# One last down product in program order: the transposes of the next layer's input moved away from their norms

## The chip, the cores and the metric

The kernel runs on one core of a Trainium2 chip. The metric is the device time of one execution in microseconds; the time given is the median of several runs. The profile is of one execution on the same core, and its times count from the first instruction of the span.

## What is computed

Two layers of a causal decoder, on x of 1024 positions by 1024 features, all in float32. Layer 0 mixes tokens by dilated window attention, layer 1 by HGRN2, a gated linear recurrence. Each mixer is followed by a dense squared-ReLU MLP, and each sub-layer is applied as a post-norm:

```python
for i in range(DEPTH):                       # 2
    y = mixer(i, x)                          # attention, then hgrn2
    x = layer_norm(ALPHA * x + y, ln_mix_g[i], ln_mix_b[i])
    y = square(relu(x @ w_up[i])) @ w_down[i]        # 1024 -> 4096 -> 1024
    x = layer_norm(ALPHA * x + y, ln_ffn_g[i], ln_ffn_b[i])
```

The change lies where the first layer's MLP ends and the second layer's mixer begins: the last part of `h @ w_down`, the layer norm, and the first products `x @ w_in` of HGRN2. ("First layer" is layer 0 in the code; the text calls the two layers 1 and 2.)

## The kernel before

Each float32 product is made of three matmuls on operands that were split into a high half (a float32r copy, by ScalarE, "ACT") and a low half (the difference, by VectorE, "DVE"): high by high, high by low and low by high. They add up in one PSUM bank. Positions are cut into eight tiles of 128, tiles 0 to 3 the first half, 4 to 7 the second.

The MLP's two products save an eighth of the work by seven block products instead of eight. In `ffn` (from L1015) the down product runs over a list `steps` (L1160): six block products, each over 16 blocks j of the hidden dimension, with four tiles at a time; and last block product 3, which is done in three passes `PASS` (L1159): tiles 0 and 1 in the first pass, tile 2 in the second, tile 3 in the third. A step of the first pass is 6 matmuls (L1260, L1263, L1264 for two tiles), one of the others 3.

For each step n the loop at L1394 writes: `load_down(n + 8)`, the loads, L1169; `product_down(n)`, the matmuls, L1249; `split_down(n + 2)`, high and low halves, L1203; and `after(n)`, L1303. For block product 3 a load at L1181 brings `d`, the hidden values of several steps at once (four steps in the first pass, eight in the others), and one at L1187 `dr`, a block of the weights, in the first pass only; the split weights `dT` are kept for the other two passes. The splits of `d` are `d3s` (L1219, L1220), in a pool of three buffers; PE frees one when a step's matmuls are done.

`after(n)` adds finished products into the residual tile z (L1282) and puts follow-up work into the list `todo`, from which the next steps take one entry each (`None` is a step without work). For a tile t the follow-up is:

- `norm_of(t)` (L1291): `ln_math` (L193): statistics and scaling on DVE, two small operations and a scaling pass on ACT (L213), the bias on GpSimd (L214, "POOL"), then the store to `x3d` (L1296), issued by the queue of SyncE ("SP").
- `tr(t)` (L1286): eight transposes of z on TensorE ("PE", L223) into two PSUM banks, and four ACT copies (L233) and four DVE differences (L234) that write the tile's columns of `xn`, the split and transposed input of the next mixer. `xn[1]` holds tiles 4 to 7, `xn[0]` tiles 0 to 3; each is a group of eight SBUF buffers, asked for at the first `tr` of its half.
- `finish(t)` (L1298): both, one after the other, in a layer that isn't the last.

The mixer that follows, `hgrn` (L1482), loads its first weights by `pre` (`gw.prefetch(0)`: L142, then the split L137, L138), clears `aT` (L1485), and runs projections of 24 matmuls (L171 to L173). The first three read `xn[1]`, the next three `xn[0]`. After each projection it takes one entry of the list `late`, which the MLP returned; before, that list is empty here.

Almost all large SBUF tiles come from one pool of 50 buffers (`U`).

What sets the order. A planner reorders the instructions of every engine: it simulates the program, gives each engine the ready instruction that is written earliest, and hands out buffers. `in_order(engines)` is the kernel's way to switch this off: between its enter and its exit each instruction on these engines is tied to the one written before it on that engine, in order only and without a wait on the chip. The up product is held so on PE, DVE and SP (L1373). For the down product `in_order(())` (L1392) names no engine, so its order is the planner's throughout.

Of the kernel before, what the change touches and what calls it, by code (L numbers as in the profile page):

```python
# [62 lines left out]
def trunk_kernel(  # L63
# [32 lines left out]
    def U(name, dt=F32):  # L96
        return up.tile([P, 1024], dt, name=name, tag="u")
# [64 lines left out]
    def new_xT(half, name):  # L162
        return XT(name)
# [23 lines left out]
    def bcast_rows(ap, name):  # L187
        t = U(name)
        nc.sync.dma_start(t, ap.rearrange("(o d) -> o d", o=1).broadcast_to([P, D]))
        return t  # L190
# [45 lines left out]
    def ln_tr(t, z, xs):  # L236
        x_ = xs[t // 4]
        c = slice((t % 4) * P, (t % 4) * P + P)
        for j, pt in enumerate(z_tr(z)):
            put(x_.hi[2 * j:2 * j + 2], x_.lo[2 * j:2 * j + 2], pt, c)  # L240
# [774 lines left out]
    def ffn(li, xf, late, res, gB_ap, bB_ap, last, pre=None):  # L1015
# [143 lines left out]
        PASS = ((0, 1), (2,), (3,))  # L1159
        steps = [(i, j, (0, 1, 2, 3)) for i in ORD for j in range(NP)]  # L1160
# [3 lines left out]
        def held(n, j):  # L1164
            if (n, j // 2) not in hold:
                hold[n, j // 2] = U("hold")
            return hold[n, j // 2][:, (j % 2) * 512:(j % 2) * 512 + 512]

        def load_down(n):  # L1169
            if n >= len(steps):  # L1170
                return
            i, j, qs = steps[n]
            top, bot = w_down[li, j], w_down[li, j + NP]
            if 0 <= n - SHIFT < NP:
                nc.sync.dma_start(held(3, n - SHIFT), w_down[li, n - SHIFT][:, R])
            if i == 3:
                w = len(qs) * P
                js = 1024 // w
                if j % js == 0:
                    many[qs] = U("d3")  # L1180
                    nc.sync.dma_start(many[qs].rearrange("p (j c) -> p j c", c=w),  # L1181
                                      hd[i - 1, j:j + js, :, qs[0] * P:qs[0] * P + w].rearrange("j p c -> p j c"))
                t = many[qs][:, j % js * w:min(j % js * w + 256, 1024)]
                r = None
                if qs == PASS[0]:
                    r = U("dr3")[:, L]
                    nc.sync.dma_start(r, bot[:, R])  # L1187
                rows_[n] = t, r
                return
            two = U("dr")  # L1190
            t, r = two[:, L], two[:, R]
            nc.sync.dma_start(t, hd[i - 1, j])
            if i == 1:
                nc.sync.dma_start(held(1, j), top[:, L])
            elif i == 6:
                nc.sync.dma_start(r, bot[:, R])
            elif i in (2, 4):
                nc.sync.dma_start(r, bot[:, L])
            rows_[n] = t, r
# [66 lines left out]
        z, sb, norm, todo = {}, {}, {}, []  # L1266

        def piece(n, q):
            if (n, q // 2) not in sb:
                sb[n, q // 2] = U("sb" + n)  # L1270
            return sb[n, q // 2][:, (q % 2) * 512:(q % 2) * 512 + 512]

        def residual(q0):
            for t in range(q0, q0 + 4):
                z[t] = U("z")
                nc.sync.dma_start(z[t], res[t * P:(t + 1) * P, :])

        def mix(t, c, other):
            v.scalar_tensor_tensor(z[t][:, c], z[t][:, c], ALPHA, other, op0=ALU.mult, op1=ALU.add)

        def plus(t, c, o):
            v.tensor_add(z[t][:, c], o, z[t][:, c])  # L1282

        xn = [None, None]

        def tr(t):  # L1286
            if xn[t // 4] is None:
                xn[t // 4] = new_xT(t // 4, f"f{li}n")
            ln_tr(t, z[t], xn)

        def norm_of(t):  # L1291
            if last:
                ln_math(z[t], norm["g"], norm["b"], out[t * P:(t + 1) * P, :])
                return
            ln_math(z[t], norm["g"], norm["b"])
            nc.sync.dma_start(x3d[t * P:(t + 1) * P, :], z[t])  # L1296

        def finish(t):  # L1298
            norm_of(t)
            if not last:  # L1300
                tr(t)

        def after(n):  # L1303
            i, j, qs = steps[n]
            x_, y_ = cur.get("x"), cur.get("y")
            if j == 8 and i == 7:
                residual(4)
            if j == 8 and i == 5:
                residual(0)
            if j == 0 and i == 4:  # L1310
                norm["g"] = bcast_rows(gB_ap, "gB")
                norm["b"] = bcast_rows(bB_ap, "bB")
            if j == NP - 1:
                if i == 1:
                    for q in range(4):
                        act(piece("p1", q), x_[q], AF.Copy)
                elif i == 6:
                    for q in range(4):
                        v.tensor_add(piece("u2", q), y_[q], piece("p1", q))
                elif i == 7:  # L1320
                    for q in range(4):
                        v.tensor_add(piece("u3", q), y_[q], piece("p1", q))
                        todo.append(lambda q=q: mix(4 + q, L, piece("p1", q)))
                        todo.append(lambda q=q: mix(4 + q, R, piece("u3", q)))
                elif i == 5:
                    for q in range(4):
                        todo.append(lambda q=q: plus(4 + q, R, x_[q]))
                        todo.append(lambda q=q: mix(q, L, piece("p1", q)))
                        todo.append(lambda q=q: mix(q, R, piece("u2", q)))
                elif i == 4:  # L1330
                    for q in range(4):
                        plus(4 + q, L, y_[q])
                        todo.extend([None, lambda q=q: norm_of(4 + q), None])
                elif i == 2:
                    for q in range(4):
                        plus(q, L, y_[q])
                    if not last:
                        for q in (4, 5):
                            todo.extend([None, None, lambda q=q: tr(q), None, None])
                        todo.extend([None] * 7)  # L1340
                    else:
                        todo.extend([None] * 17)
                elif qs == PASS[0]:
                    for q in qs:
                        plus(q, R, x_[q])
                    if last:
                        todo.extend([None, lambda: finish(0), None, None, None, None, lambda: finish(1), None])
                    else:
                        todo.extend([None, lambda: tr(6), None, lambda: finish(0), None, None, None,
                                     lambda: tr(7), None, lambda: finish(1), None, None, None])  # L1350
                elif qs == PASS[1]:
                    plus(qs[0], R, x_[qs[0]])
                    todo.extend([None, lambda: finish(2)])
                    if pre:
                        todo.append(pre)
                else:
                    plus(qs[0], R, x_[qs[0]])
                    while todo:
                        f = todo.pop(0)
                        if f:  # L1360
                            f()
                    finish(qs[0])
            elif todo:
                f = todo.pop(0)
                if f:
                    f()
# [6 lines left out]
        order = in_order((mybir.EngineType.PE, mybir.EngineType.DVE, mybir.EngineType.SP, ))  # L1373
# [15 lines left out]
        low_up()  # L1389
        sum_up(4)  # L1390
        order.__exit__()
        order = in_order(())  # L1392
        order.__enter__()
        for n in range(len(steps)):  # L1394
            load_down(n + LOADDN)
            product_down(n)
            split_down(n + SPLITDN)
            if n + SPLIT3 < len(steps) and len(steps[n + SPLIT3][2]) == 1:
                split_down(n + SPLITDN + 1)
                split_down(n + SPLIT3)  # L1400
            after(n)
        order.__exit__()
        return xn, []


    def hgrn_consts():
# [75 lines left out]
    def hgrn(xs, late, consts, pre, gw):  # L1482
# [103 lines left out]
        for hd in range(8):  # L1586
# [66 lines left out]
            if hd == 0:  # L1653
                new = [[]] + new
            pend = [(pend[i] if i < len(pend) else []) + (new[i] if i < len(new) else [])
                    for i in range(max(len(new), len(pend)))]
# [14 lines left out]
    hc = hc[0]  # L1671
    gw = GateW()
    xs, late = ffn(0, xf, late, x1d, ln_ffn_g[0], ln_ffn_b[0], False, lambda: gw.prefetch(0))
    pr = Out(w_hgrn_out, "h", 1)
    oN, fill = hgrn(xs, late, hc, pr.pre, gw)
    xf, late = outproj_ln(pr, oN, fill, lambda t: x3d[t * P:(t + 1) * P, :],
                          ln_mix_g[1], ln_mix_b[1], x5d)
    ffn(1, xf, late, x5d, ln_ffn_g[1], ln_ffn_b[1], True)


# [75 lines left out]
```

## Time and profile before

| what | value |
|---|---|
| median of 3 runs | 2849.05 us |
| lowest and highest run | 2847.23 and 2850.16 us |
| the profiled execution | 2848.19 us |
| its span, first to last instruction | 2846.4 us |
| busy share of the span: PE, DVE, ACT, POOL | 97%, 73%, 51%, 4% |
| mean granted TensorE clock | 0.996 of full |
| layer 1's last block product and the first 30 matmuls of the mixer | 1693.93 to 1763.85 us of the span |

The profile has the busy time of each engine over the span, in 40 slices, by groups of instructions and in windows of choice; the timeline of each engine; its waits, with the instruction that ended each; and the SP queue, which issues the loads and stores. A row of the timeline is start, length, engine, line, operation, output and inputs, then `x` and a count, where several in a row are merged, and in brackets the idle time just before with what ended it. "PEld" is the weight load of a matmul, which overlaps other matmuls. Matmuls follow each other faster than their shown length, since they are pipelined.

### The profile page before, as it was taken

How to read it: one execution, taken by the hardware profiler on the slowest of the kernel's cores; microseconds unless marked ns; L12 is line 12 of the kernel's file. 1: busy time of each engine (PE TensorE's matmuls, PEld its weight loads, DVE VectorE, ACT ScalarE, POOL GpSimd, SP SyncE). 2: the span in 40 equal slices, each digit the busy share in tenths (PEclk: the TensorE clock that was granted, in tenths of full speed). 3: DMA queues.
4: the chain of work that ended last, by engine and by line, in shares of the span. 5: the costliest groups of instructions: out<-in, count | busy, mean ns of one | idle time of the engine just before them, and what ended most of it. 6: DMA issues, size and time to landing. Idle time of an engine off the chain costs nothing.

```text
span 2846.4 us, 40146 instructions
## 1 busy us (share of the span) xinstructions
PE 2773.5 (97%) x14280; PEld 2229.2 (78%) x14280; DVE 2065.6 (73%) x3830; ACT 1449.9 (51%) x3105; POOL 122.7 (4%) x67
## 2 busy tenths in 40 slices
PE   8999999999999989999999998999999999999998
PEld 6777777777777767888878887787887788878887
DVE  7768777776877767786686875565667787678677
ACT  5555555655555555544454434555553545454433
POOL 0000000000000003100000011111102200000000
PEclk9999999999999999999999999999999999999999
DMA  7766665766667523464483843001132455475654
GB/s 287 255 199 194 187 203 171 216 202 206 189 197 226 161 80 133 152 218 159 163 313 124 268 158 104 33 35 60 53 119 80 150 203 175 159 270 188 223 174 133
DMA packets 204936, 485.27 MB, mean 170 GB/s; under 512 B 29376, under 2 KB 43712, under 8 KB 204736
## 3 DMA queue, kind: packets, MB, share of 16 engines
q1 hardware_dynamic: 204736, 482.72, 51.3%
q8 instruction: 112, 1.84, 0.3%
q14 instruction: 88, 0.72, 0.1%
HBM read 362.82 MB, written 94.24 MB: 161 GB/s over the span
## 4 chain that ended last, share of the span: by engine, by line
PE 85%; DVE 6%; issue 3%; ACT 3%; DMA 2%; POOL 1%; SPq 0%; DVEq 0%; POOLq 0%; ACTq 0%
PE pmm L666 8%; PE pmm L668 8%; PE pmm L667 8%; PE pup L1114 7%; PE pup L1112 7%; PE pup L1113 7%; PE pdy L1260 4%; PE pdy L1264 4%; PE pdy L1263 4%; PE pdx L1263 3%; PE pdx L1264 3%; PE pdx L1260 3%; PE s L500 3%; PE o L539 2%; PE ppt L524 2%
## 5 line engine op out<-in xcount | busy, mean ns | idle before, releaser
L666 PE MATMUL pmm<-xh,H 128*128 128x512 f32 x1008 | 407.3, 404 | 13.1 <-ACT H L432 8.8
L668 PE MATMUL pmm<-xh,H 128*128 128x512 f32 x1008 | 395.6, 392 | 0.2 <-DVE H L440 0.2
L667 PE MATMUL pmm<-xl,H 128*128 128x512 f32 x1008 | 395.3, 392 | 0.0
L666 PEld LDWEIGHTS pmm<-xh,H 128*128 128x128 f32 x1008 | 190.8, 189 | 53.4 <-ACT H L432 8.8
L668 PEld LDWEIGHTS pmm<-xh,H 128*128 128x128 f32 x1008 | 189.9, 188 | 42.3 <-DVE H L440 0.9
L667 PEld LDWEIGHTS pmm<-xl,H 128*128 128x128 f32 x1008 | 190.9, 189 | 36.6
L514 ACT ACTIVATE p<-p,stats 128x128 f32<-128x128 f32 (+1 forms) x384 | 168.3, 441 | 93.6 <-DVE stats L511 93.1
L1263 PE MATMUL pdy<-dT,dS 128*128 128x512 f32 x512 | 199.2, 389 | 0.0
L1260 PE MATMUL pdy<-dT,dS 128*128 128x512 f32 x512 | 199.2, 389 | 0.0
L1264 PE MATMUL pdy<-dT,dS 128*128 128x512 f32 x512 | 199.2, 389 | 0.0
L511 DVE CUSTOM_DVE_ANT_0 p<-s,mask 128x128 f32<-128x128 f32 (+1 forms) x384 | 113.2, 347 | 67.7 <-PE s L500 58.4
L137 ACT ACTIVATE dS<-dr 128x512 fp32r<-128x512 f32 x192 | 119.6, 623 | 72.7 <-PE pdy L1264 36.6
L171 PE MATMUL pmm<-f0nh,wh 128*128 128x512 f32 x384 | 153.1, 399 | 0.0
L173 PE MATMUL pmm<-f0nh,wl 128*128 128x512 f32 x384 | 149.8, 390 | 0.0
L172 PE MATMUL pmm<-f0nl,wh 128*128 128x512 f32 x384 | 149.7, 390 | 0.0
L138 DVE TENSOR_TENSOR dS<-dr,dS 128x512 fp32r<-128x512 f32 x192 | 135.0, 703 | 16.1 <-ACT dS L137 12.3
L214 POOL TENSOR_TENSOR z<-z,bB 128x1024 f32<-128x1024 f32 x24 | 58.5, 2442 | 1686.6 <-ACT z L213 1679.8
L527 ACT ACTIVATE pts<-ppt 128x256 f32<-128x256 f32 (+1 forms) x192 | 85.4, 474 | 62.3 <-PE ppt L524 60.1
L137 ACT ACTIVATE dT<-hold 128x512 fp32r<-128x512 f32 x128 | 80.0, 625 | 69.1 <-DVE hold L1239 28.8
L1073 ACT ACTIVATE H<-wc 128x512 fp32r<-128x512 f32 x128 | 77.2, 625 | 74.6 <-DVE wc L1066 43.9
L1264 PEld LDWEIGHTS pdy<-dT,dS 128*128 128x128 f32 x512 | 96.1, 188 | 20.1
L1263 PEld LDWEIGHTS pdy<-dT,dS 128*128 128x128 f32 x512 | 96.1, 188 | 19.9
(395 smaller groups left out, 6943.3 us busy)
## 6 DMA issues: line engine op xcount, KB each, us to landing
xh<-xtd SPq DMA_DIRECT2D x110, 512.0 KB
xl<-xtd SPq DMA_DIRECT2D x110, 512.0 KB
dr<-hd SPq DMA_DIRECT2D x192, 256.0 KB
dr<-in_w_down_dram SPq DMA_DIRECT2D x128, 256.0 KB
rot<-e SPq DMA_DIRECT2D x192, 128.0 KB
wa<-in_w_up_dram SPq DMA_DIRECT2D x48, 512.0 KB
wb<-in_w_attn_dram SPq DMA_DIRECT2D x36, 512.0 KB
wa<-in_w_attn_dram SPq DMA_DIRECT2D x33, 512.0 KB
```

The costliest lines, as they stand in the source:

```text
L137: act(hi, raw, AF.Copy)
L171: nc.tensor.matmul(o, wh[:, k], xs.h(k), start=k == 0, stop=False)
L514: act(p[:, h, :n], p[:, h, :n], AF.Exp, bias=sS[:, 0, h, b:b + 1], scale=-1.0, accum_out=sS[:, 1, h, b:b + 1])
L666: nc.tensor.matmul(o, wh, hi[k // 2][:, c], start=begin and k == 0, stop=False, skip_group_check=True)
L667: nc.tensor.matmul(o, wh, lo[k // 2][:, c], start=False, stop=False, skip_group_check=True)
L668: nc.tensor.matmul(o, wl, hi[k // 2][:, c], start=False, stop=end and k == 3, skip_group_check=True)
L1112: nc.tensor.matmul(o, wh, xf.h(b, k), start=begin and k == 0, stop=False, skip_group_check=True)
L1113: nc.tensor.matmul(o, wh, xf.l(b, k), start=False, stop=False, skip_group_check=True)
L1114: nc.tensor.matmul(o, wl, xf.h(b, k), start=False, stop=end and k == 3, skip_group_check=True)
L1260: nc.tensor.matmul(o[q], h, T_[:, L], start=begin, stop=False, skip_group_check=True)
L1263: nc.tensor.matmul(o[q], h, T_[:, R], start=False, stop=False, skip_group_check=True)
L1264: nc.tensor.matmul(o[q], l, T_[:, L], start=False, stop=end, skip_group_check=True)
```

## The change

Three things, all in the first of the two layers; the program of the last layer is the same as before.

1. From the first step of block product 3's first pass, PE runs in program order. The exit of that region isn't at the end of the MLP: it is handed to the mixer as the third entry of `late`, and so comes behind the mixer's third projection.
2. `finish` is taken apart for tiles 0 to 3. The norms stay where they were. The transposes of tiles 0 and 1 move from the second pass into the third (behind its steps 3 and 8), with `pre` between them (behind step 4 instead of 3).
3. The transposes of tiles 2 and 3, which were in the third pass and behind it, become the first two entries of `late`: they come behind the mixer's first and second projection.

```diff
@@ after(n), at the end of the first pass @@
-                        todo.extend([None, lambda: tr(6), None, lambda: finish(0), None, None, None,
-                                     lambda: tr(7), None, lambda: finish(1), None, None, None])
+                        todo.extend([None, lambda: tr(6), None, lambda: norm_of(0), None, None, None,
+                                     lambda: tr(7), None, lambda: norm_of(1), None, None, None])
                 elif qs == PASS[1]:
                     plus(qs[0], R, x_[qs[0]])
-                    todo.extend([None, lambda: finish(2)])
-                    if pre:
-                        todo.append(pre)
+                    if last:
+                        todo.extend([None, lambda: finish(2)])
+                    else:
+                        todo.extend([None, lambda: norm_of(2), lambda: tr(0), pre, None, None, None, lambda: tr(1)])
                 else:
                     plus(qs[0], R, x_[qs[0]])
                     while todo:
                         f = todo.pop(0)
                         if f:
                             f()
-                    finish(qs[0])
+                    norm_of(qs[0])
@@ the loop over the steps @@
-        order = in_order(())
-        order.__enter__()
+        order = in_order((mybir.EngineType.PE,))
         for n in range(len(steps)):
+            if not last and steps[n] == (3, 0, PASS[0]):
+                order.__enter__()
             load_down(n + LOADDN)
             product_down(n)
             split_down(n + SPLITDN)
...
             after(n)
-        order.__exit__()
-        return xn, []
+        if last:
+            return
+        return xn, [lambda: tr(2), lambda: tr(3), order.__exit__]
```

## The prediction

> **What bounds the kernel now.** I read the page's busy shares first, then the stretch that the change touches in windows, then what PE waits for there, then the SP queue. Times are us from the start of the span.
>
> ```profile
> PE 2773.5 (97%) x14280; PEld 2229.2 (78%) x14280; DVE 2065.6 (73%) x3830; ACT 1449.9 (51%) x3105; POOL 122.7 (4%) x67
> ```
> ```profile
> 1693.93:1719.07 25.14, 24.43 (x113) 19.56 (x112) 19.09 (x41) 13.98 (x34) 0.00 (x0) 1.00 0.18 53
> 1719.07:1733.46 14.39, 13.11 (x65) 10.40 (x63) 9.79 (x27) 7.35 (x19) 4.91 (x3) 1.00 0.10 38
> 1733.46:1754.51 21.05, 16.70 (x73) 13.08 (x73) 15.82 (x32) 12.24 (x27) 3.07 (x2) 0.84 0.62 199
> 1754.51:1763.85 9.34, 7.81 (x39) 6.29 (x38) 4.48 (x8) 2.29 (x5) 2.36 (x1) 1.00 0.01 5
> 1763.85:1800.62 36.77, 36.77 (x165) 30.45 (x164) 13.04 (x13) 16.90 (x22) 5.44 (x2) 1.00 0.24 85
> ```
> ```profile
> 2794.21:2837.74 43.53, 43.53 (x192) 35.85 (x191) 1.97 (x3) 0.00 (x0) 1.00 0.27 79
> ```
>
> PE is busy 97% of the span, so it is the bound, and a change like this can only win PE's holes. The rows after the page's line give length, then busy time of PE, PE's weight loads, DVE, ACT and POOL, then granted clock, DMA share and GB/s (the last row, restricted to the product's bank, has no POOL). They are layer 1's last down product: first pass (16 steps of 6 matmuls), second and third pass (16 steps of 3 each), then the mixer's first 30 matmuls and the 162 after them. The last row is the same product in layer 2: 192 matmuls without a hole in 43.53, that is 0.2267 each. The mixer's are as fast (36.77 / 162 = 0.2270).
>
> ```profile
> 1698.02 1.03 PE L223 MATMUL lnpt<-ident,z 128*128 128x128 f32 x8
> 1698.81 0.48 PE L1260 MATMUL pdx<-dT,d3s 128*128 128x512 f32 x1
> ...
> 1702.08 0.73 PE L1260 MATMUL pdx<-dT,d3s 128*128 128x512 f32 x2 [0.18 <-ACT dT L137]
> ...
> 1703.84 0.71 PE L223 MATMUL lnpt<-ident,z 128*128 128x128 f32 x5
> 1705.08 0.73 PE L1260 MATMUL pdx<-dT,d3s 128*128 128x512 f32 x2 [0.53 <-ACT dT L137]
> ...
> 1730.97 1.09 PE L223 MATMUL lnpt<-ident,z 128*128 128x128 f32 x8 [1.28 <-POOL z L214]
> ...
> 1739.00 0.80 PE L1260 MATMUL pdx<-dT,d3s 128*128 128x512 f32 x1 [2.00 <-ACT d3s L137]
> ...
> 1748.10 1.10 PE L223 MATMUL lnpt<-ident,z 128*128 128x128 f32 x8 [0.84 <-POOL z L214]
> ...
> 1763.00 1.09 PE L223 MATMUL lnpt<-ident,z 128*128 128x128 f32 x8 [1.53 <-POOL z L214]
> ```
>
> One tile's eight transposes push the next matmul back by 0.79, and by 0.85 with the slightly longer gap behind it. So the time lost in each stretch is its length less its work: first pass 25.14 - 96 x 0.2267 - 2 x 0.85 = **1.7**; second 14.39 - 48 x 0.2267 - 2 x 0.85 = **1.8**; third 21.05 - 48 x 0.2267 - 3 x 0.85 = **7.6**; mixer 9.34 - 30 x 0.2267 - 0.85 = **1.7**. Together 12.8 us: all that can be won here. Tiles 0, 2 and 3 are transposed at 1730.97, 1748.10 and 1763.00, each while PE waits for POOL to finish that tile's norm: the transposes stand too close behind their norms. The largest hole is another one, the third pass's first step at 1739.00, where PE waits for the split of data that came late. The SP queue says why:
>
> ```profile
> 1690.58 6.19 SPq L1181 DMA_DIRECT2D d<-hd  x2
> 1730.94 2.68 SPq L1296 DMA_DIRECT2D x3d<-z  x2
> 1733.71 1.47 SPq L1181 DMA_DIRECT2D d<-hd  x2
> 1735.23 1.34 SPq L142 DMA_DIRECT2D wr<-in_w_hgrn_dram  x1
> ...
> 1748.07 0.33 SPq L1296 DMA_DIRECT2D x3d<-z  x1
> 1748.49 0.38 SPq L142 DMA_DIRECT2D wr<-in_w_hgrn_dram  x1
> ```
> ```profile
> 1733.71 4.80 DMA d<-hd
> ```
>
> SP stands for 34 us (from 1690.58 + 6.19 to 1730.94) at the store of tile 0, which waits for POOL; the third pass's two loads and the mixer's first weights are queued behind it. The load then takes 4.80 (the last row, from the chain of waits), to 1738.5, and its split releases PE at 1739.00.
>
> **The change part by part.** No work is added or dropped: 192 matmuls, 64 transposes, the same norms, stores and loads. Only order changes.
>
> *Tiles 0 and 1.* Their transposes leave the second pass for steps 3 and 8 of the third. Tile 0's is then due 9 matmuls into the third pass. Both norms need the end of the first pass, as before. Before, the first pass ended at 1719.07 and POOL released tile 0 just before 1730.97, 11.9 later; tile 1 needs one more POOL add of 2.4 (two in 4.71):
>
> ```profile
> 1728.55 4.71 POOL L214 TENSOR_TENSOR z<-z,bB 128x1024 f32<-128x1024 f32 x2 [47.71 <-ACT z L213]
> 1733.20 0.95 POOL L1485 MEMSET aT<- 128x1024 f32 x1
> ```
> ```profile
> L234 DVE TENSOR_TENSOR f0nl<-lnpt,f0nh 128x256 fp32r<-128x256 f32 x28 | 11.2, 419 | 6.5 <-ACT f0nh L233 6.3
> L138 DVE TENSOR_TENSOR wl<-wr,wh 128x1024 fp32r<-128x1024 f32 x3 | 3.7, 1222 | 0.7 <-ACT wh L137 0.6
> ```
>
> Now PE needs 48 x 0.2267 + 2 x 0.85 = 12.6 for the second pass and 2.0 for nine more matmuls, so it asks for tile 0 at 14.6 and for tile 1 at 14.6 + 0.85 + 3.4 = 18.9 after the first pass, where they are there at 11.9 and 14.3. The 1.28 goes. What is late next: tile 7's transposes return to their written place in the second pass, which puts 4 x 0.42 = 1.7 us of DVE in front of the norms. The margins of 2.7 and 4.6 cover it.
>
> *Tiles 2 and 3.* Tile 2 is transposed behind the mixer's first projection, tile 3 behind the second. Norm of 2 begins at the second pass's end and took 14.6 there (1733.46 to 1748.07, its store); it is now needed 12.6 (third pass with two tiles) + 24 x 0.2267 = 18.0 later. Norm of 3 took 8.5 (1754.51 to 1763.00) and is needed 2 x 5.4 + 0.85 = 11.7 after the third pass. The 0.84 and 1.53 go.
>
> *The loads.* This is the largest term and it is not in the diff. The new tile group (xn[0], eight buffers of the pool of 50) is first written by the split of tile 0's transposes. In the old text that stands ahead of the third pass's loads (they are written at step 9 of the second pass and step 1 of the third), in the new text behind both (step 3 of the third). The trace bears out that buffers are given in program order:
>
> ```profile
> 1682.83 1.14 ACT L137 ACTIVATE dT<-dr 128x512 fp32r<-128x512 f32 x2
> ...
> 1701.41 0.62 ACT L137 ACTIVATE dT<-dr 128x512 fp32r<-128x512 f32 x1
> ```
>
> POOL idles for 47.71, yet the memset of aT, which waits for no data, comes only when tile 0 is out; and ACT has a hole between the dT of the fifth step (last at 1682.83) and that of the sixth (1701.41), the first that is written behind tile 4's transposes and their group xn[1]. So I expect the loads beside the second pass's at about 1697, long before they are needed. Bounds: from 0, like layer 2's row, to a wait as long as now, worked out under the first rival. I take 0.
>
> *The pin.* In the first pass PE today fills its waits for ACT's dT with tile 5's transposes (the last five at 1703.84) and runs two L1260 ahead of the low half. In program order tile 5 comes after 48 matmuls, not 36, and L1263 must follow its own L1260. PE then meets the same dT at 1705.1 with tile 5 still to do: 0.85, and some 0.3 for the lost swaps. Cost 1.1, between 0 (if ACT, replanned, is earlier) and 2. The first pass then loses 1.7 + 1.1 = 2.8.
>
> *DVE in the third pass.* Norm of 2, two tiles' splits (3.4), eight d3s (3.4) and a weight's low half (1.22) make some 13 us in a stretch of 12.6. Layer 2's row (no wait, without transposes) is one end, 0; the other is a late split or weight, 3. I take 1.5 for this, the second pass and the first projection together, nearer to the row.
>
> *The weights.* wr is still behind tile 0, transposed at 1693.93 + 26.3 + 12.6 + 2.0 = about 1735; issue 1736, landing 4.1 later, then 1.06 + 1.22: 1742.5. The 4.1 is a later weight's time from its issue at 1748.49 to its split, which the DMA released:
>
> ```profile
> 1752.57 1.06 ACT L137 ACTIVATE wh<-wr 128x1024 fp32r<-128x1024 f32 x1 [0.51 <-DMA wr<-in_w_hgrn_dram]
> ```
> The first projection is due about 1746, so this is covered by some 3.5 us; without that cover each us would cost one.
>
> **Sum.** 12.8 lost now, 2.8 + 1.5 = 4.3 then: **8.5 us won**. What follows runs without a hole for 36.77 us and is moved as a whole. The profiled execution took 2848.19 (span 2846.4), so 2839.7; the median of the runs is 0.86 above it, and there the forecast is **2840.5**.
>
> The clock, by its row:
>
> ```profile
> 1736.50:1743.40 6.90, 4.90 (x16) 3.68 (x15) 4.17 (x11) 3.36 (x11) 0.00 (x0) 0.51 1.09 361
> ```
>
> Eight matmuls and eight transposes in it ran at half speed, some 2.3 of the third pass's 7.6 (8 x 0.2267, and 0.5 for the transposes); the forecast has no such stretch. The Trainium skill (TensorE: Matmul & The Clock Gate, Part 1) says that an idle window of about 3.4 us halves the clock, and its Part 4 that transposes do not count as busy. The longest hole here is 2.00, but between the matmuls of 1733.46 and 1739.00 lie 5.5 us with transposes alone, so the trace agrees with both together and not with Part 1 alone. By Part 1 alone a wait in the first rival would cost its length only; by both together, the 2.3 as well.
>
> **The rivals.** *The loads stay behind the stores* (the queue order of today). PE ends the second pass at about 1733 and waits until 1739.0: 5.9, and 2.3 of clock. The gain is 8.5 - 8.2, time 2849, within 0.2%. For it: SP's order is replanned and tile 0's store still has the earlier place in the text. Against: two loads written earlier than both came at 1690.58.
>
> *The mixer's weights fall behind tile 2's store*, the slower side. If the buffers for wr come only when tile 2 is out (14.6 after the second pass, 1747.7), they land at 1752, PE stands from 1746 to 1753 (7), pays 2.3 for the clock and 2 more when the second weight queues behind tile 3's store: 8.5 - 11.3, time about 2852; with the mixer's own waits for outputs (7.2, below) half as long again, about 2855. It decides from an issue of wr later than about 1746; each us later costs one. Against: today wr goes out 4 us after tile 0's transposes and 13 ahead of tile 2's store.
>
> *Half of it*: the plan of the mixer, which is not pinned and where PE now waits 7.2 us for transposes of the outputs, falls out worse by some us, or DVE is late by 3 and more. Gain 3 to 5, about 2845.
>
> ```profile
> PE opt L1568 <- DVE on L1560: 7.2, 5, 1.5
> ```
>
> **How the numbers follow.** Forecast 0.62; loads behind the stores 0.10; half of it 0.14; weights late 0.14, of which 0.10 with the mixer's longer waits. A measurement of this kernel tells about 0.2% (5.7 us) from no change: the forecast lies beyond it, the half, the queue rival and the late weights alone within. So faster 0.62 + 0.02 (the upper end of the half) = 0.64, same 0.10 + 0.12 + 0.04 = 0.26, slower 0.10. The range goes from 2835.5 (all 12.8 won, little more) to 2849.0 (the queue rival); what is left out is the late weights and a part of the unforeseen on either side.
>
> **What would show it.** Right: third-pass loads issued near 1697; no wait for POOL z at L223 in this stretch; the clock at 1.00 throughout; PE waiting for dT for 2 to 3 us in the first pass; the 72nd mixer matmul done near 1765 instead of 1773.4. Wrong: tile 0's store ahead of the loads, a wait at L171 for wh or wl, or new waits for DVE in the mixer. The whole forecast falls if buffers are not given in program order.

## The result, and the profile after

The changed kernel takes **2844.65 us** (median of 20 runs, 2842.86 to 2846.46), the kernel before 2848.45 beside it (20 runs): ratio 0.9986, 95% interval 0.998 to 0.9992. It is faster by 3.8 us, or 0.14%, where 8.5 were forecast. The time lies inside the range, and the sign was right. But the forecast, and nearly all of the 0.64 for "faster", meant a gain beyond 0.2%, and the result lies within 0.2%.

The profiled execution took 2844.54 (span 2842.8). First the page's line of busy times, then the same four stretches in windows: length, busy PE, weight loads, DVE, ACT and POOL, granted clock, DMA share, GB/s. The last window here ends with the mixer's 72nd matmul.

```profile
PE 2772.0 (98%) x14280; PEld 2229.9 (78%) x14280; DVE 2068.6 (73%) x3830; ACT 1449.2 (51%) x3105; POOL 122.7 (4%) x67
```
```profile
1694.09:1719.20 25.11, 24.44 (x113) 19.52 (x112) 19.13 (x41) 14.02 (x34) 0.00 (x0) 1.00 0.33 95
1719.20:1731.87 12.67, 12.67 (x65) 10.66 (x64) 11.17 (x29) 7.99 (x22) 3.23 (x2) 1.00 0.01 1
1731.87:1750.02 18.15, 14.77 (x66) 11.71 (x64) 13.07 (x24) 7.60 (x18) 4.76 (x3) 0.91 0.54 202
1750.02:1770.07 20.05, 18.42 (x89) 15.09 (x88) 11.42 (x18) 8.51 (x16) 2.37 (x1) 1.00 0.35 132
```

The prediction's formula (length less 0.2267 per matmul and 0.85 per tile, two tiles in each window) gives what each loses:

| stretch | before | forecast | after |
|---|---|---|---|
| first pass | 1.7 | 2.8 | 1.7 |
| second pass | 1.8 | with the next two: 1.5 | 0.1 |
| third pass | 7.6 | | 5.6 |
| mixer, first three projections | 1.7 | | 2.0 |
| sum | 12.8 | 4.3 | 9.3 |

So 3.5 us came out of the stretch, and 3.8 out of the time: what follows moved as a whole. The gain that is missing lies in the third pass and the first projections. PE's waits over the whole stretch (us in all, times, longest) and the rows of its timeline at the holes name them:

```profile
PE lnpt L223 <- DVE f0nl L234: 2.1, 1, 2.1
PE pmm L173 <- DVE wl L138: 1.6, 1, 1.6
PE pdx L1264 <- DVE d3s L138: 1.2, 1, 1.2
...
```
```profile
1733.72 0.50 PE L1264 MATMUL pdx<-dT,d3s 128*128 128x512 f32 x1 [1.23 <-DVE d3s L138]
...
1739.74 0.60 PE L223 MATMUL lnpt<-ident,z 128*128 128x128 f32 x4
1742.48 0.63 PE L223 MATMUL lnpt<-ident,z 128*128 128x128 f32 x4 [2.14 <-DVE f0nl L234]
...
1743.64 0.51 PE L1260 MATMUL pdx<-dT,d3s 128*128 128x512 f32 x1
...
1747.29 0.40 PE L1260 MATMUL pdx<-dT,d3s 128*128 128x512 f32 x1
...
1758.60 0.49 PE L173 MATMUL pmm<-f0nh,wl 128*128 128x512 f32 x1 [1.63 <-DVE wl L138]
```

No transpose waits for POOL any more; the three large holes are all waits for DVE. Yet DVE is busy for only 13.07 of the third pass's 18.15. Its own rows and POOL's, side by side, say why:

```profile
1728.64 4.74 POOL L214 TENSOR_TENSOR z<-z,bB 128x1024 f32<-128x1024 f32 x2 [47.66 <-ACT z L213]
1739.35 2.36 POOL L214 TENSOR_TENSOR z<-z,bB 128x1024 f32<-128x1024 f32 x1 [5.97 <-ACT z L213]
...
1755.09 2.37 POOL L214 TENSOR_TENSOR z<-z,bB 128x1024 f32<-128x1024 f32 x1 [12.48 <-ACT z L213]
```
```profile
1730.45 0.76 DVE L234 TENSOR_TENSOR f0nl<-lnpt,f0nh 128x256 fp32r<-128x256 f32 x2 [0.83 <-ACT f0nh L233]
1731.12 2.88 DVE L138 TENSOR_TENSOR d3s<-d,d3s 128x256 fp32r<-128x256 f32 x2
...
1739.92 2.08 DVE L138 TENSOR_TENSOR d3s<-d,d3s 128x256 fp32r<-128x256 f32 x1
1741.92 0.41 DVE L234 TENSOR_TENSOR f0nl<-lnpt,f0nh 128x256 fp32r<-128x256 f32 x1
...
1756.05 2.50 DVE L138 TENSOR_TENSOR wl<-wr,wh 128x1024 fp32r<-128x1024 f32 x1 [2.23 <-ACT wh L137]
```

A split of d normally takes 0.42. The one that starts under POOL's first pair of adds is shown for some 2.5 and ends about 0.3 after them (they end at 1733.38); another starts at 1739.92 under the next add and ends at 1742.00, also 0.3 after it (1741.71). A weight's split takes 2.50 where 1.22 is usual. "Busy" here is standing still. The differences f0nl keep their 0.4 even under POOL's adds (two in 0.76 at 1730.45): of their inputs one lies in PSUM, while both inputs of a d3s or wl lie in SBUF. The f0nl for which PE waited 2.14 had only queued behind a d3s.

The trace of before already showed this, in its third pass, under tile 2's add (POOL, DVE, and the splits of d as a group with the shortest, the median and the longest in ns):

```profile
1745.67 2.37 POOL L214 TENSOR_TENSOR z<-z,bB 128x1024 f32<-128x1024 f32 x1 [11.52 <-ACT z L213]
```
```profile
1745.93 3.07 DVE L138 TENSOR_TENSOR d3s<-d,d3s 128x256 fp32r<-128x256 f32 x3 [0.21 <-ACT d3s L137]
```
```profile
L138 DVE TENSOR_TENSOR d3s<-d,d3s x14: 406/414/2398, 1719.9 to 1751.1; 128x256 fp32r<-128x256 f32 x14
```

Three splits in 3.07 are one of 2.4 and two of 0.4. There one split was held; after the change the loads are earlier, the splits of the third pass with them, and two of d and one of a weight are held.

The Trainium skill (SBUF — State Buffer, Who interferes with whom) states this as an exclusive lock: a VectorE instruction with two SBUF inputs contends with a GpSimd instruction that reads SBUF, and the later one is blocked for the other's whole length. The traces here agree (0.42 becomes 2.08 to 2.5). It is the rule that spoke against this change, and the prediction didn't weigh it.

The SP queue after:

```profile
1690.49 12.79 SPq L1181 DMA_DIRECT2D d<-hd  x4
1731.08 10.98 SPq L1296 DMA_DIRECT2D x3d<-z  x3
1742.15 0.38 SPq L142 DMA_DIRECT2D wr<-in_w_hgrn_dram  x1
```

All four loads of d are issued by 1703.3 (1690.49 + 12.79; the forecast said about 1697), 30 us sooner than before and ahead of the stores. The mixer's weights went behind tile 2's store, as the slower rival had it, but at 1742.15 already, and PE ran the first projection without a wait for them.

### The profile page after: what moved, and what is told of

The parts are those of the page before. It is cut to its first block, busy times and chain, and to the rows that moved or that the text cites. A ratio compares the mean times of both kernels' runs of the same rounds, so it can differ in the third digit from the quotient of the medians.

```text
span 2842.8 us, 40144 instructions
## 1 busy us (share of the span) xinstructions
PE 2772.0 (98%) x14280; PEld 2229.9 (78%) x14280; DVE 2068.6 (73%) x3830; ACT 1449.2 (51%) x3105; POOL 122.7 (4%) x67
```

## The experiments

**Theory:** POOL's bias adds hold DVE's two-input splits, and through them PE. **Rivals:** DVE simply has too much to do between these norms; or program order keeps PE from filling its waits; and the small gain that there is may come from the loads alone. The measure beside the time is the length from the first pass's first matmul to the mixer's 72nd in each kernel's own trace, which is one execution: 79.56 before, 75.98 after. The work in it is 264 x 0.2267 + 8 x 0.85 = 66.65, the rest is lost. Ratios are against the kernel before on the same chip.

| kernel | time (runs) | ratio, 95% | stretch | lost |
|---|---|---|---|---|
| after | 2844.65 (20) | 0.9986, 0.998 to 0.9992 | 75.98 | 9.3 |
| e1_dve_bias | 2839.60 (5) | 0.9966, 0.9954 to 0.9979 | 70.30 | 3.7 |
| e2_quarters | 2843.73 (11) | 0.9979, 0.9971 to 0.9988 | 74.02 | 7.4 |
| e3_no_pin | 2842.19 (10) | 0.9976, 0.9967 to 0.9986 | 72.40 | 5.8 |
| e4_loads_early | 2844.38 (10) | 0.9983, 0.9974 to 0.9992 | 74.74 | 8.1 |
| e5_pin_only | 2869.28 (2) | 1.007, 1.0051 to 1.0088 | 97.28 | 30.6 |
| e6_pin_second | 2845.45 (10) | 0.9988, 0.9979 to 0.9997 | 76.05 | 9.4 |
| e7_dve_no_pin | 2839.68 (5) | 0.9965, 0.9953 to 0.9978 | 69.77 | 3.1 |
| e8_late_t4 | 2837.98 (5) | 0.9962, 0.9948 to 0.9976 | 68.79 | 2.1 |
| e9_idle_pool | 2847.22 (11) | 0.9991, 0.9982 to 1.0 | 77.79 | 11.1 |
| e10_all_dve | 2833.81 (5) | 0.9948, 0.9935 to 0.996 | 68.76 | 2.1 |
| e11_no_pin_again | 2842.07 (7) | 0.9974, 0.9963 to 0.9985 | 72.82 | 6.2 |
| e12_after_again | 2845.51 (11) | 0.9988, 0.9979 to 0.9996 | 74.88 | 8.2 |

**e1_dve_bias**: the change, with the bias of tiles 0 to 3 on DVE (one pass for scale and bias), so that POOL adds nothing here. DVE has more to do, ACT and POOL less.

```diff
-        act(z, z, AF.Copy, scale=w[:, 3:4])
-        nc.gpsimd.tensor_add(z, z, bB)
+        nc.vector.scalar_tensor_tensor(z, z, w[:, 3:4], bB, op0=ALU.mult, op1=ALU.add)
```

> The changed kernel, with the bias of the norms of tiles 0 to 3 added by DVE (one pass z*w+b of some 1.28 us) in place of ACT's scaling and POOL's add. Theory 1 (DVE's split, which reads two SBUF operands, is held up while POOL's add runs): no d3s split longer than 0.5 us and no wl split longer than 1.3 between 1719 and 1760, the waits of 1.2, 2.1 and 1.6 us on DVE go, the TensorE clock stays at 1.00; the third pass loses about 1 us instead of 5.6 and the mixer's first three projections 0.5 instead of 2.0; 4 to 6 us faster than the changed kernel, about 2839 to 2840. Theory 2 (DVE simply has too much to do in the second and third pass): 4 x 1.28 us more on DVE make the waits longer; 2846 to 2849.

2839.60, and 5.7 us less stretch than after. The splits of d (min, median and longest in ns) and PE's waits:

```profile
L138 DVE TENSOR_TENSOR d3s<-d,d3s x17: 407/418/426, 1715.2 to 1742.2; 128x256 fp32r<-128x256 f32 x17
```
```profile
PE lnpt L223 <- DVE f0nl L234: 1.4, 1, 1.4
...
```

No split is held, and with four passes more, 1.28 each in its timeline, DVE makes PE wait once only, for 1.4, where the three waits were 5.0 together: it hadn't too much to do. Lost are 1.7 in the first pass and 0.1, 1.7 and 0.1 in the others. The third pass was expected at about 1; the wait of 1.4 is at tile 1's transposes, where the changed kernel had its 2.14, so not all of that hole need be the held split's. This kernel also has a shorter norm, so it can't say alone which of the two won.

**e9_idle_pool** separates the add itself from its place in the norm: as e1, and POOL makes the same adds into a spare buffer that nobody reads. No transpose waits for it; the spare buffer is one of the pool's 50, and z is freed only behind the add.

```diff
+        nc.vector.scalar_tensor_tensor(z, z, w[:, 3:4], bB, op0=ALU.mult, op1=ALU.add)
+        nc.gpsimd.tensor_add(spare, z, bB)
```

> As the kernel with the bias of tiles 0 to 3 on DVE, but POOL runs the same four adds of z and b beside it, into a spare buffer that nobody reads and nobody waits for. Theory 1 (DVE's split with two SBUF operands is held up while POOL's add runs): splits of 1.5 us and more come back and PE waits for DVE again, 1 to 3 us together; 2840.5 to 2843. If what DVE's bias won was only the shorter chain of the norm, the splits stay at 0.42 and 1.23 and the time at 2839 to 2840.

2847.22, 7.6 above e1 (7.1 by the ratios): in the theory's direction, and worse than the 2840.5 to 2843 that it expected. POOL, DVE and PE:

```profile
1728.34 2.40 POOL L214 TENSOR_TENSOR spare<-z,bB 128x1024 f32<-128x1024 f32 x1 [47.35 <-DVE z L213]
1734.54 2.68 POOL L214 TENSOR_TENSOR spare<-z,bB 128x1024 f32<-128x1024 f32 x1 [3.80 <-DVE z L213]
1741.64 2.34 POOL L214 TENSOR_TENSOR spare<-z,bB 128x1024 f32<-128x1024 f32 x1 [4.42 <-DVE z L213]
...
1758.99 3.25 POOL L214 TENSOR_TENSOR spare<-z,bB 128x1024 f32<-128x1024 f32 x1 [14.12 <-DVE z L213]
```
```profile
1728.78 2.25 DVE L138 TENSOR_TENSOR d3s<-d,d3s 128x256 fp32r<-128x256 f32 x1
...
1734.89 0.69 DVE L196 BATCH_NORM_STATS2 lnst<-z 128x6 f32<-128x512 f32 x1
1735.50 2.00 DVE L138 TENSOR_TENSOR d3s<-d,d3s 128x256 fp32r<-128x256 f32 x1
...
1741.41 0.42 DVE L234 TENSOR_TENSOR f0nl<-lnpt,f0nh 128x256 fp32r<-128x256 f32 x1
1741.75 2.52 DVE L138 TENSOR_TENSOR d3s<-d,d3s 128x256 fp32r<-128x256 f32 x1
...
1758.76 1.22 DVE L138 TENSOR_TENSOR wl<-wr,wh 128x1024 fp32r<-128x1024 f32 x1
```
```profile
1745.08 1.09 PE L223 MATMUL lnpt<-ident,z 128*128 128x128 f32 x4 [4.00 <-DVE f0nl L234]
```

Under each of the first three adds one split is held until the add ends; the statistics (one SBUF input) right under the second take their usual 0.69. With the fourth it is the other way round: the weight's split starts 0.23 before the add, takes its usual 1.22, and the add is shown for 3.25 instead of 2.4. So the one that starts later is held, whichever engine it is on. Behind the third add PE stands for 4.00, and the clock falls (0.84 in the third pass): eleven matmul starts from 1746.39 to 1750.95 take 4.56 instead of 11 x 0.2267 = 2.49, so some 2 us of the difference in this execution are the clock. Adds whose result nobody uses cost some 7 us, and the splits that they hold stand right ahead of PE's waits: the theory is shown. What the spare buffer costs the planner by itself was not measured.

**e2_quarters**: the change, with POOL's add in four adds of 256 columns.

```diff
+        [nc.gpsimd.tensor_add(z[:, c], z[:, c], bB[:, c]) for c in (four slices of 256)]
```

> The changed kernel, with POOL's add of tiles 0 to 3 cut into four adds of 256 columns. Theory 1 (held up for as long as one POOL instruction runs): the longest d3s split of this stretch falls from 2.4 us to about 1.1 (0.42 plus one quarter of some 0.6), the three waits on DVE shrink from 5.0 us together to under 2.5; 1.5 to 3 us faster than the changed kernel, 2841.5 to 2843. Theory 2 (too much work on DVE): DVE has the same work, so splits and waits are as before, 2844 to 2845.5.

```profile
L138 DVE TENSOR_TENSOR d3s<-d,d3s x19: 408/426/950, 1714.9 to 1744.5; 128x256 fp32r<-128x256 f32 x19
```
```profile
PE pmm L171 <- ACT wh L137: 1.8, 1, 1.8
PE lnpt L223 <- POOL z L214: 1.4, 1, 1.4
PE pmm L173 <- DVE wl L138: 1.2, 2, 0.6
```

The longest split falls from 2.5 to 0.95, as theory 1 expected (1.1): a split gets in between two adds. But four adds take longer than one (3.21 for tile 2 in its timeline, 2.36 in one piece), and PE now waits for POOL and for a weight's high half. The time lies between the ranges of the two theories, and its interval overlaps that of after, so no gain from shorter adds is shown. The lengths of the splits decide for theory 1, the time doesn't.

**e3_no_pin, e11_no_pin_again**: the change with the planner's order on PE. **e12_after_again**: the change once more, beside e11.

```diff
-        order = in_order((mybir.EngineType.PE,))
+        order = in_order(())
```

> The changed kernel without the pin: the planner is free on PE as before, the transposes are written in their new places. If the gain comes from where the transposes are written (and the loads that thereby pass the stores), it stays: SP issues the third pass's loads near 1691 to 1703, time 2843 to 2846. If the pin makes it, the time is that of the kernel before, 2848.5. The first pass should lose what it loses with the pin, 1.7 us, within 0.3.

> The changed kernel without the pin once more, beside the changed kernel on one chip. If the pin costs by itself, 1.5 to 3.5 us less than the changed kernel; if the earlier difference was scatter, the same within 1 us.

> The changed kernel once more, as the partner of the run without the pin: 2844 to 2845.5 with the before at 2848.5, and the slow clock of 3.4 us in the third pass again if it belongs to the order and not to chance.

2842.19 and 2842.07 without the pin, 2844.65 and 2845.51 with it: the pin costs some 3 us, not where I looked for it. The waits of e3:

```profile
PE lnpt L223 <- DVE f0nl L234: 1.7, 1, 1.7
PE pdx L1264 <- DVE d3s L138: 1.2, 1, 1.2
...
```

The two holes of the third pass stay; the 1.63 for wl in the mixer is gone, since in this order no weight's split lies under an add. So of the 3 us some 1.6 to 1.8 are that hole (lost in the mixer 2.0 and 2.5 with the pin, 0.5 and 0.7 without). The rest isn't settled. The intervals of 0.9988 and 0.9974 overlap by a little, but of e11's seven runs six are below the fastest of e12's eleven (2844.43), on one chip.

**e7_dve_no_pin**: e1 without the pin.

> The bias of tiles 0 to 3 on DVE, transposes in their new places, no pin. If the pin costs by itself (3.6 us shorter without it in one profile), this is faster than with the pin, by 1 to 3 us: 2836.5 to 2838.5. If the unpinned order was only better at dodging POOL's adds, which are gone here, it is the same as with the pin, 2839 to 2840, the stretch within 1 us of 70.3.

2839.68, the same as e1. Without POOL's adds the order of PE makes no difference that these runs show: the pin's harm goes with the holes that they make.

**e6_pin_second**: the change, pinned from the second pass on.

```diff
-            if not last and steps[n] == (3, 0, PASS[0]):
+            if not last and steps[n] == (3, 0, PASS[1]):
```

> The changed kernel with the pin from the second pass on, so that the planner may again draw tile 5's transposes into the first pass's waits. By the prediction's step the pin costs 1.1 us in the first pass, so the first pass would lose 0.5 to 0.6 less than it does now if that cover were worth it; the changed trace shows the same 1.7 lost with and without, so: first pass 1.7 within 0.2, time 2843.5 to 2845.5, that of the changed kernel.

Nothing won. The first pass takes 25.14 unpinned, 25.11 pinned:

```profile
1694.81:1719.95 25.14, 24.43 (x114) 19.56 (x112) 19.10 (x41) 13.97 (x34) 0.00 (x0) 1.00 0.32 93
```

**e5_pin_only**: the places of before, with the pin.

> The kernel before with the pin alone: PE in program order over the same region, the transposes in their old places, right behind their norms. PE must then stand for most of each norm: tile 0 due 18 matmuls and one tile (4.9 us) into the second pass and there after 11.9, tiles 2 and 3 behind chains of 10 to 14 and 8.5 us; holes of some 7, 9 and 8 us, each with a slow clock behind it. SP order as before. 2866 to 2878, 18 to 29 slower than before. If the pin and not the places were what wins, 2845.

```profile
PE lnpt L223 <- POOL z L214: 21.3, 3, 7.7
```

2869.28 where the kernel before took 2848.11 on the same chip: transposes in program order right behind their norms wait out three norms. The moves are what makes the pin bearable.

**e4_loads_early**: the kernel before; only the third pass's loads are written earlier, at the first step of the second pass, ahead of xn[0].

```diff
+            if not last and n == 112:
+                for m in range(128, 144):
+                    load_down(m)
```

> The kernel before, with the third pass's two loads written at the first step of the second pass, ahead of tile 0's norm and transposes; nothing else. If buffers are given in program order and the loads stood behind tile 0's group, SP issues them by 1703 instead of 1733.7, the wait of 2.00 us at the third pass's first step goes, and with it most of the slow clock: 2 to 4 us faster than before, 2844.5 to 2846.5. The splits now have their data while POOL adds, so one split of 2 us or more should appear in the second pass (theory 1). If the loads were held by something else, nothing changes: 2848.5.

```profile
1692.73 12.62 SPq L1181 DMA_DIRECT2D d<-hd  x4
1733.16 2.86 SPq L1296 DMA_DIRECT2D x3d<-z  x2
1736.12 0.38 SPq L142 DMA_DIRECT2D wr<-in_w_hgrn_dram  x1
```
```profile
PE lnpt L223 <- POOL z L214: 3.5, 3, 1.3
PE lnpt L223 <- DVE f0nl L234: 1.6, 1, 1.6
...
```

Written ahead of xn[0], the loads go out some 30 us sooner, the hole of 2.00 and the slow clock behind it are gone, and the time is that of the whole change: the loads alone can give all that the change gave. The waits for POOL stay, as they should. Theory 1 also expected a held split in the second pass: two splits there, under the adds of tiles 0 and 1, take 3.89 together (the longest 2.6), and a later one under tile 2's add 1.91. PE waits for none of them directly, but the wait of 1.6 is for a difference that stands right behind the first two in DVE's order.

**e8_late_t4**: e1, with tile 4's transposes, the first that ask for xn[1], moved from an early step of the first pass to step 14, and tile 5's to step 2 of the second.

```diff
-                        for q in (4, 5):
-                            todo.extend([None, None, lambda q=q: tr(q), None, None])
-                        todo.extend([None] * 7)
+                        todo.extend([None] * 13)
+                        todo.extend([lambda: tr(4), None, None, lambda: tr(5)])
```

> The pinned kernel with the bias on DVE, and tile 4's transposes written at step 14 of the first pass instead of step 3, tile 5's at step 2 of the second. If buffers are given in program order, the splits dT of steps 6 to 16 no longer stand behind the group that tile 4 opens, and the first pass loses under 0.5 us instead of 1.7: 1 us faster, 2838 to 2839, unless the second pass, with three tiles now, loses it again. If dT is late for its loads, the first pass loses 1.7 as before.

```profile
1692.60:1715.25 22.65, 22.65 (x105) 18.85 (x104) 17.39 (x36) 12.72 (x29) 0.95 (x1) 1.00 0.39 106
```

The first pass loses 22.65 - 96 x 0.2267 - 0.85 = 0.04 instead of 1.7. ACT's splits dT, which ACT's timeline of after shows only from 1701.55 on, behind the copies into xn[1], start at 1694.48 here. ACT's copies for tiles 4 and 5 are later here too, but before them ACT stood idle for 11.54 in after (up to 1695.65), so it wasn't ACT's work that held the splits: this fits buffers given in program order, as e4 does.

**e10_all_dve**: e8, with the bias on DVE in all 24 norms whose bias POOL adds.

> The kernel with late transposes of tile 4 and the bias on DVE, and the bias of all other 20 POOL adds of the norms on DVE too. Where DVE has room this shortens each norm by some 2 us and frees its splits from POOL's adds; where the output products are fed by DVE it adds 1.28 us for each tile. PE waits little in those stages, so I expect 0 to 2 us won, 2836 to 2838.

2833.81 (2832.02 to 2838.72): ratio 0.9948, faster than the kernels before and after the change, and below the 2836 to 2838 expected. Its stretch is that of e8. Whether the other 20 norms gain anything isn't shown: the ratio's interval overlaps that of e8, and the execution whose trace was taken is the slowest, 2838.72.

## Why the prediction was half right

**The loads**: right. Issued by 1703.3, no wait at the third pass's first step, and by e4 and e8 for the reason given. **Tiles 0 to 3**: right; the waits of 1.28, 0.84 and 1.53 for POOL are gone. **What follows**: right; in all kernels but e5 and e10 the stretch and the time differ from before by the same to about 1.3 us.

**The pin**: mis-sized and misplaced. In the first pass it cost 0 instead of 1.1 (25.11 against 25.14), and PE waited 0.7 there for dT, not 2 to 3. It costs in the mixer, where PE in program order meets a weight's split under POOL's add.

**DVE in the third pass**: the step that failed. "I take 1.5", with 3 as the end, for the second pass, the third and the first projection; measured 0.1 + 5.6 + 2.0 = 7.7 (the 2.0 includes the second and third projections, for which the prediction put nothing; the 1.63 lies in the second). It added up splits of 0.42 and 1.22, their durations on a free DVE, and has no term for POOL's adds beside them. Of the 7.7, 1.23 + 2.14 + 1.63 = 5.0 are holes behind held splits (how much of the 2.14 would be there without, is open), and 1.6 is the clock below. Without the adds (e1) the same terms are 0.1 + 1.7 + 0.1 = 1.9: the sum of DVE's work was about right, the hold was missing from it. What made it worse is the step that was right: the loads put the splits of d ahead in time, under the adds of tiles 0 to 2.

That the time still lies in the range is in part luck. The stretch lost 9.3 instead of 4.3: some 6.2 more for DVE, and 1.1 less because the pin's cost in the first pass didn't come.

**The clock**: no slow stretch was forecast. Behind the 2.14 hole, with only transposes between the matmuls on its two sides, the profiled execution had one:

```profile
1743.80:1747.20 3.40, 3.40 (x10) 2.61 (x9) 1.37 (x4) 1.44 (x4) 0.00 (x0) 0.50 0.99 337
```

Nine matmul starts from 1743.64 to 1747.29 take 3.65 instead of 9 x 0.2267 = 2.04: 1.6 us. The same program in e12 has the same three holes and no such stretch (1.00 throughout), so it comes with some executions only. The matmuls on the two sides are 3.0 us apart (1739.50 + 0.39 to 1742.86) in both traces, less than the idle window that the prediction names. The Trainium skill (TensorE: Matmul & The Clock Gate, Part 1) says that the window is free-running and its effect varies from run to run; the two traces agree.

**The weights**: their queue did fall behind tile 2's store, the mechanism of the slower rival, but before the 1746 from which it was said to decide, and it cost nothing. **Half of it** was given 2845 "or DVE is late by 3 and more", and that is what happened; its chance of 0.14 was too low, since the held split in the trace of before (2.4 among 0.4) is not in its working.

## What to carry to other kernels

Look at the longest of a group, not only its mean: one split of 2.4 in a group of fourteen with a median of 0.41 was the clue, and the row of another engine at the same time gave its reason. An engine that is busy 4% can still hold up the one that feeds the bound; in this kernel a bias add was cheaper on a VectorE that had room than on GpSimd beside two-input splits. When a transfer or a split is moved forward, ask what it will then run beside.

## What was not expected of the hardware

- A DVE subtraction with both inputs in SBUF stands still while POOL adds from SBUF: 0.42 becomes 1.9 to 2.6, a weight's 1.22 becomes 2.50. One with an input in PSUM doesn't (0.4). If a two-input split starts first, it is POOL's add that takes longer (3.25 instead of 2.4). The trace books the time as busy. With POOL's add in quarters the longest is 0.95.
- The clock fell to half for 3.4 us behind a hole of 2.14 in one execution and stayed at full in another with the same holes.
